# Meta tokens loaded eight tiles wide, x in eight pieces, and residual rows stored block by block from GpSimd's queue

## The chip, the cores and the metric

The kernel runs on one core of one Trainium2 chip. A core has five engines that run their own instruction streams: TensorE (PE; its weight loads are listed as PEld), VectorE (DVE), ScalarE (ACT), GpSimd (POOL) and SyncE (SP). SP issues nearly all loads; POOL and ACT can issue transfers too. They are carried by the core's 16 DMA engines. The metric is device time of one launch, in microseconds (us), lower is better. A profiled execution also gives a span, from its first to its last instruction.

## What is computed

One layer of a decoder trunk: 16 learned meta tokens are put ahead of 256 tokens of x (width 2048), and the layer's output for the 256 is returned. All data are float32.

```python
h = jnp.concatenate([meta_b, x], axis=1)            # 16 + 256 tokens, 2048 wide
u = rms_norm(h, g_pre_mix[l])
proj = u @ w_in[l]                                  # 2048 x 7168
z_pool, v_conv, g_conv, gate_a, gate_b = jnp.split(proj, splits, axis=-1)
y_a = causal_multiscale_pool(z_pool, w_pool_grp[l], pool_scale[l]) @ w_pool_out[l]
y_b = conformer_conv(v_conv, g_conv, w_dw[l], b_dw[l], conv_ln_g[l], conv_ln_b[l]) @ w_conv_out[l]
m = jax.nn.sigmoid(gate_a) * y_a + jax.nn.sigmoid(gate_b) * y_b
h = h + rms_norm(m @ w_o[l], g_post_mix[l])
u = rms_norm(h, g_pre_mlp[l])
f = jnp.square(jax.nn.relu(u @ w_up[l])) @ w_down[l]
h = h + rms_norm(f, g_post_mlp[l])
return h[:, N_META:]
```

## The kernel before

**Numbers in two parts.** TensorE multiplies float32 in a faster form with fewer bits, so every operand is kept as a high and a low part: ScalarE casts the number into `hi`, VectorE subtracts that from the number and leaves `lo`. A product of two operands then takes three matmuls (high by high, high by low, low by high). Weights arrive in rooms of 1 MB called `raw...`, are split into `hi` and `lo`, and are then multiplied; when the split is done, the room is free for the next load.

**The start (L427 to L596).** The token matrix is transposed on TensorE, because a product needs the width on the partitions. `x_in` holds x as two groups of 128 tokens; `x_tile(k)` (L484) transposes 128 columns of both groups and ScalarE and VectorE turn them into the two parts of `u`, scaled by `g_pre_mix`. `meta_tiles` (L495) does the same for the meta tokens, whose rows are in `m_in`, 16 partitions of 2048 numbers: one thin transpose for each of the 16 column tiles. The result `mt` is multiplied on VectorE, and the first part of it is cast on ScalarE before x's first tile.

The first product takes the weights of 256 columns over all 2048 rows, 16 steps `k`, and runs while x and the weights still arrive. `turn_and_split(k)` (L575) issues one tile of x and one piece of weights; three tiles (`LEAD`) are turned before the first step, and each step turns the one that comes three later. Between them stand dummy transposes (`keep_warm`, L449) that write a bank nobody reads; `DUMMIES` gives their numbers, 11 ahead of everything, 2 behind the meta tokens and 1 behind the three tiles.

SP's queue is first in, first out. `X_BEHIND` (L427) says behind which rows of which weight chunk a block of x is loaded: x's first 512 columns come at once, in two pieces on two queues (L436), and three blocks of 512 follow.

On GpSimd's queue a copy (L442) waits for the last block of x; behind it stand the conv taps and the rows of small vectors, which TensorE transposes at L904.

**The middle.** Two planned stretches follow. `Plan` (L47) collects work items with an engine, a cost and the names they read and write, simulates them, and issues them in that order. The first planned stretch ends with the product by `w_o`.

**From h to the up product (L1566 to L1681).** This part is written out by hand. `norm1.finish` gives the factor of the first norm, `residual(t, n)` (L1500) writes block `n` (512 columns) of token group `t` of the new residual `h1`, in place over the copy of x loaded there. `u2_tiles` (L1571) transposes tiles of `h1` and ScalarE and VectorE split them; `up_high` and `up_low` multiply them by the first weights of `w_up`. The scale of the second norm is not yet known then; it is applied later, by `rb`.

**The second planned stretch (from L1722).** It needs the sum of squares of `h1` (`square_h1`, eight activations on ScalarE) and gives the room of `h1` to weights, so `h1` is first stored to memory, to be read back for the last residual:

```python
    def keep_h1():
        nc.sync.dma_start(kept, h1)
        room = big.tile([P, len(H_ROOMS), CK * CW], F32, tag="k8", bufs=2, name="raw_h1")
        for n, r in enumerate(H_ROOMS):
            room_of[r] = room[:, n, :]
```

The loads into rooms 5 and 6 (`raw_h1`) stand behind this store.

## Time and profile before

| what | us |
|---|---|
| median of 3 runs | 1182.91 |
| lowest and highest of them | 1181.70, 1183.52 |
| profiled execution, its own time | 1181.75 |
| its span | 1179.6 |
| mean granted TensorE clock in it | 0.997 |

In the views, a line names the source line, the engine, the operation, the tile written and the tiles read (buffer numbers left out), the shape and the count; then busy time and mean length of one. In a timeline the first two numbers are start and length in us, and the bracket is how long the engine had stood idle before and what released it. In a table of stretches the first number after the limits is the length, then come the busy time and number of instructions of PE, PEld, DVE, ACT and POOL, the granted clock, the share of the DMA engines that was busy, and GB/s. In a list of transfers the last number is the median time in us from issue to landing.

### The profile page before, as it was taken

The page shows a single profiled execution, that of the slowest core. Times are in us where ns is not written, and L with a number is a line of the kernel's source. Part 1 is how long each engine was busy: PE and PEld are TensorE (multiplying, and loading weights), DVE is VectorE, ACT ScalarE, POOL GpSimd, SP SyncE. Part 2 cuts the span into 40 slices and gives each one's busy share as a digit, 9 for nine tenths or more (in the row PEclk, how much of TensorE's full clock was granted, in tenths as well). Part 3 has the DMA queues.
Part 4 walks back from the last instruction along what each step waited for, and adds up shares of the span by engine and source line. Part 5 has one row for each costly group of instructions (what it writes and reads, how often), then busy time and mean ns, then how long its engine had stood idle before and what let it go on. Part 6 is the DMA issues. An engine that isn't in the chain of part 4 may idle for free.

```text
span 1179.6 us, 15795 instructions
## 1 busy us (share of the span) xinstructions
PE 1167.2 (99%) x6314; PEld 1013.1 (86%) x6314; DVE 1064.4 (90%) x1155; ACT 706.8 (60%) x718; POOL 62.3 (5%) x62
## 2 busy tenths in 40 slices
PE   9999999999999999999999999999999999999996
PEld 9999998788888888898888888888888888888885
DVE  6799999999998998688998998998989989989857
ACT  7634454556478666566776666666656756656542
POOL 1000000000000000000101001000000010010000
PEclk9999999999999999999999999999999999999998
DMA  9855356789767799449999999999999999999941
GB/s 316 265 179 179 108 179 173 233 278 297 220 194 247 208 353 293 151 149 347 253 320 234 249 316 256 250 290 244 301 262 229 339 240 248 318 241 242 337 143 71
DMA packets 185177, 287.57 MB, mean 244 GB/s; under 512 B 4769, under 2 KB 92257, under 8 KB 184192
## 3 DMA queue, kind: packets, MB, share of 16 engines
q1 hardware_dynamic: 160784, 236.40, 58.7%
q0 software_dynamic: 23856, 49.44, 23.3%
q8 instruction: 49, 0.80, 0.3%
q10 hardware_dynamic: 464, 0.73, 0.2%
q14 instruction: 24, 0.20, 0.0%
HBM read 282.36 MB, written 4.19 MB: 243 GB/s over the span
## 4 chain that ended last, share of the span: by engine, by line
PE 95%; DVE 3%; DMA 1%; issue 1%; ACT 0%; DVEq 0%; ACTq 0%
PE bank_u L539 18%; PE bank_k L1252 16%; PE acc_up L1979 13%; PE bank_u L545 9%; PE acc_v L1252 9%; PE bank_k L534 8%; PE bank_a L1979 7%; PE bank_b L1979 5%; PE acc_v L534 4%; PE acc_up L539 1%; DVE lo L822 1%; PE bank_u L1979 1%; PE acc_up L545 1%; DMA raw_k<-in_w_in_dram 1%; PE acc_v L1512 0%
## 5 line engine op out<-in xcount | busy, mean ns | idle before, releaser
L539 PE MATMUL bank_u<-m,hi 128*128 128x512 f32 x960 | 329.6, 390 | 0.0
L545 PE MATMUL bank_u<-m,lo 128*128 128x256 f32 x960 | 265.3, 276 | 0.0
L539 PEld LDWEIGHTS bank_u<-m,hi 128*128 128x128 f32 x960 | 180.2, 188 | 38.0
L817 ACT CAST hi<-raw_p 128x2048 fp32r<-128x2048 f32 x70 | 133.8, 1912 | 111.1 <-PE bank_k L1252 28.2
L1805 DVE TENSOR_TENSOR lo<-raw_m,hi 128x2048 fp32r<-128x2048 f32 x75 | 171.6, 2288 | 18.5 <-ACT hi L1800 17.3
L545 PEld LDWEIGHTS bank_u<-m,lo 128*128 128x128 f32 x960 | 180.2, 188 | 1.6
L1800 ACT CAST hi<-raw_m 128x2048 fp32r<-128x2048 f32 x75 | 143.5, 1913 | 60.8 <-PE bank_u L539 39.3
L822 DVE TENSOR_TENSOR lo<-raw_p,hi 128x2048 fp32r<-128x2048 f32 x70 | 159.7, 2286 | 12.9 <-ACT hi L817 12.6
L1979 PE MATMUL acc_up<-hi,forms 128*128 128x512 f32 x440 | 143.9, 390 | 0.0
L1805 DVE TENSOR_TENSOR lo<-raw_h,hi 128x2048 fp32r<-128x2048 f32 x43 | 98.4, 2288 | 12.7 <-ACT hi L1800 12.3
L1800 ACT CAST hi<-raw_h 128x2048 fp32r<-128x2048 f32 x43 | 82.2, 1911 | 39.9 <-PE bank_u L539 17.7
L952 DVE SCALAR_TENSOR_TENSOR c<-a,taps,c 128x256 f32<-128x256 f32 x240 | 100.2, 478 | 0.0
L1979 PEld LDWEIGHTS acc_up<-hi,forms 128*128 128x128 f32 x440 | 82.6, 188 | 18.1 <-ACT G L2004 0.4
L534 PE MATMUL bank_k<-u_um,hi 128*128 128x272 f32 x512 | 95.2, 287 | 0.0
L1252 PE MATMUL bank_k<-hi,u_um 128*128 128x512 f32 x280 | 88.8, 389 | 0.7 <-ACT sg L1301 0.7
L1979 PE MATMUL acc_up<-lo,forms 128*128 128x512 f32 x220 | 86.0, 391 | 0.0
L1979 PE MATMUL bank_a<-hi,forms 128*128 128x512 f32 (+1 forms) x256 | 81.9, 383 | 0.0
L534 PEld LDWEIGHTS bank_k<-u_um,hi 128*128 128x128 f32 x512 | 79.7, 188 | 0.0
L534 PE MATMUL bank_k<-u_um,lo 128*128 128x272 f32 x256 | 73.3, 287 | 0.0
L1800 ACT CAST hi<-raw_c 128x2048 fp32r<-128x2048 f32 x23 | 43.9, 1908 | 41.7 <-PE bank_u L539 36.8
L1805 DVE TENSOR_TENSOR lo<-raw_c,hi 128x2048 fp32r<-128x2048 f32 x23 | 52.6, 2287 | 13.2 <-ACT hi L1800 13.2
L1979 PE MATMUL bank_b<-hi,forms 128*128 128x512 f32 (+1 forms) x200 | 63.5, 381 | 0.0
(398 smaller groups left out, 2230.6 us busy)
## 6 DMA issues: line engine op xcount, KB each, us to landing
raw_p<-in_w_in_dram SPq DMA_DIRECT2D x30, 1024.0 KB, 5.6
raw_m<-in_w_down_dram SPq DMA_DIRECT2D x25, 1024.0 KB, 8.8
raw_m<-in_w_down_dram POOLq DMA_DIRECT2D x23, 1024.0 KB, 10.2
raw_h<-in_w_up_dram SPq DMA_DIRECT2D x20, 1024.0 KB, 8.3
raw_m<-in_w_up_dram SPq DMA_DIRECT2D x17, 1024.0 KB, 8.2
raw_h<-in_w_down_dram SPq DMA_DIRECT2D x17, 1024.0 KB, 9.0
raw_c<-in_w_down_dram SPq DMA_DIRECT2D x15, 1024.0 KB, 5.2
raw_k<-in_w_in_dram SPq DMA_DIRECT2D x14, 1024.0 KB, 8.2
```

Of the source, the lines that this page charges most:

```text
L534: nc.tensor.matmul(acc, w[:, k[0], cs], act[:, k[1], a, off:], start=first and n == 0, stop=last and n == 2)
L539: nc.tensor.matmul(acc.rearrange("p (a t) -> p a t", a=2)[:, :, ts], hi[:, k[0], cs], act[:, k[1], :, off + ts.start:off + ts.stop], start ...
L545: nc.tensor.matmul(acc[:, :T], lo[:, k[0], cs], act[:, k[1], 0, off:], start=False, stop=stop, skip_group_check=True)
L817: nc.scalar.copy(box["flat"], rooms[q]())
L822: nc.vector.tensor_sub(lo, rooms[q](), f32(box["flat"]))
L952: nc.vector.scalar_tensor_tensor(C_c()[:, q, :], A_a()[:, q, i:i + T], taps[:, q, i:i + 1], C_c()[:, q, :], op0=ALU.mult, op1=ALU.add)
L1252: nc.tensor.matmul(banks[bank], a_(k, part), box[w_][:, k, :], start=opens and k == 0 and i == 0, stop=ends_ and k == CK - 1 and i == 2, s ...
L1800: nc.scalar.copy(box["flat"], raw_in(room))
L1805: nc.vector.tensor_sub(lo, raw_in(room), f32(box["flat"]))
L1979: nc.tensor.matmul(acc, forms[h][:, f, k, a_, :], box[w_][:, k, cs], start=start and k == 0 and n == 0, stop=stop and k == KH - 1 and n == ...
```

## The change

Four things change.

1. The meta tokens are loaded a second way, `m_wide`: 128 partitions that hold 8 column tiles of 16 tokens each, twice. Two full transposes replace sixteen thin ones. `m_in` is still needed for the squares; it is now loaded on GpSimd's queue, ahead of the taps, and its squares come behind all those of x.
2. x is loaded in blocks of 256 columns: the first in two pieces, seven more behind two rows of weights each.
3. Two tiles of x are turned before the first step of the first product, and two more (the third and fourth) behind it. The dummies become 12 at the start and 3 ahead of the first step.
4. `h1` is stored in five pieces from GpSimd's queue, each as soon as its blocks are written, and six of its eight squares are issued by hand between the transposes. The planned stretch has no store, and the loads into its two rooms wait for the last two squares in the plan alone.

```diff
-DUMMIES = (11, 2, 1)
+DUMMIES = (12, 3)
...
-    X_BEHIND = {(0, 4): 1, (0, 8): 2, (1, 4): 3}
+    X_COLS = CW // 2
+    X_BEHIND = {(0, 2): 1, (0, 4): 2, (0, 6): 3, (0, 8): 4, (1, 2): 5, (1, 4): 6, (1, 6): 7}
...
-    nc.sync.dma_start(m_in, meta)
+    KM = P // M
+    m_wide = tmp.tile([P, KD // KM, P], F32, tag="v", bufs=5, name="m_wide")
+    nc.sync.dma_start(m_wide, meta.rearrange("m (c k p) -> k m c p", k=KM, p=P))
     pre_rows = load_rows(nc.scalar, "g_pre_mix")
     for t, queue in enumerate((nc.scalar, nc.sync)):
-        queue.dma_start(x_in[:, t, :CW], xv[:, t, :CW])
+        queue.dma_start(x_in[:, t, :X_COLS], xv[:, t, :X_COLS])
...
+    nc.gpsimd.dma_start(m_in, meta)
     nc.gpsimd.dma_start(taps_in, w_dw)
...
-        pt = acc_tile("mt_in")[:, :KD * M].rearrange("p (k m) -> p k m", k=KD)
-        for k in range(KD):
-            nc.tensor.transpose(pt[:, k, :], m_in[:, k * P:(k + 1) * P], ident[:M, :M])
+        pt = acc_tile("mt_in")[:, :KD * M]
+        for c in range(KD // KM):
+            nc.tensor.transpose(pt[:, c * P:(c + 1) * P], m_wide[:, c, :], ident)
+        pt = pt.rearrange("p (k m) -> p k m", k=KD)
...
-    squares = [(b, t) for b in range(XB) for t in range(NT + 1)]
+    squares = [(b, t) for b in range(XB) for t in range(NT)] + [(b, NT) for b in range(XB)]
...
     meta_parts.pop(0)()
+    for k in range(2):
+        turn_and_split(k)
     keep_warm(DUMMIES[1])
-    for k in range(LEAD):
-        turn_and_split(k)
-    keep_warm(DUMMIES[2])
...
-        turn_and_split(k + LEAD)
+        for n in range(2 if k == 0 else k + LEAD, k + LEAD + 1):
+            turn_and_split(n)
...
+    def square_h1(t, n):
+        square_of(h1[:, t, block(n)], ssq2, t, n)
+
+    def keep(t, n0, n1):
+        cs = slice(n0 * CW, n1 * CW)
+        nc.gpsimd.dma_start(kept[:, t, cs], h1[:, t, cs])
...
     for n in range(2):
         residual(0, n)
+    square_h1(0, 0)
+    keep(0, 0, 2)
     last_block(0)
...
     residual(0, 2)
+    keep(0, 2, 3)
...
     both(u2_tiles(0, 1, 2 * CK, CK))
+    square_h1(0, 1)
     up_high(1, 0)
     parts_ = u2_tiles(1, 1, 0, CK)
     residual(1, 1)
+    keep(1, 0, 2)
     both(parts_)
+    square_h1(0, 2)
     up_high(2, 0)
     both(u2_tiles(1, 1, CK, CK))
+    for n in range(2):
+        square_h1(1, n)
     residual(1, 2)
+    square_h1(1, 2)
     last_block(1)
     residual(1, 3)
     residual(0, 3)
+    keep(1, 2, 4)
+    keep(0, 3, 4)
...
-    def keep_h1():
-        nc.sync.dma_start(kept, h1)
+    def rooms_of_h1():
         room = big.tile([P, len(H_ROOMS), CK * CW], F32, tag="k8", bufs=2, name="raw_h1")
...
     for t in range(NT):
-        for n in range(NB):
-            plan.add("ACT", 0.92, square_h1(t, n), writes=("junk", "ssq2"))
-    plan.add("SP", 6.0, keep_h1, reads=("ssq2",), writes=[f"raw{r}" for r in H_ROOMS])
+        plan.add("ACT", 0.92, lambda t=t: square_h1(t, NB - 1),
+                 reads=[f"raw{r}" for r in H_ROOMS], writes=("junk", "ssq2"))
```

The order of instructions at three places. First TensorE's start, before the change (`idle` are dummies, `xt` tiles of x, `acc_v` the first product):

```order
L451 MATMUL idle<-ident 128x128 x11
L421 MATMUL pv_g_pre_mix<-ident,rows_g_pre_mix 128x16
L498 MATMUL mt_in<-ident,m_in 128x16 x16
L451 MATMUL idle<-ident 128x128 x2
L488 MATMUL xt_175<-ident,x_in 128x128 x2
L488 MATMUL xt_182<-ident,x_in 128x128 x2
L488 MATMUL xt_189<-ident,x_in 128x128 x2
L451 MATMUL idle<-ident 128x128
L534 MATMUL acc_v_0_169<-u_um,hi_83 128x272 x2
```

And TensorE's start with the change:

```order
L455 MATMUL idle<-ident 128x128 x12
L421 MATMUL pv_g_pre_mix<-ident,rows_g_pre_mix 128x16
L502 MATMUL mt_in<-ident,m_wide 128x128 x2
L492 MATMUL xt_166<-ident,x_in 128x128 x2
L492 MATMUL xt_173<-ident,x_in 128x128 x2
L455 MATMUL idle<-ident 128x128 x3
L539 MATMUL acc_v_0_162<-u_um,hi_83 128x272 x2
L539 MATMUL acc_v_0_162<-u_um,lo_80 128x272
L539 MATMUL acc_v_1_163<-u_um,hi_83 128x272 x2
L539 MATMUL acc_v_1_163<-u_um,lo_80 128x272
L492 MATMUL xt_189<-ident,x_in 128x128 x2
L492 MATMUL xt_196<-ident,x_in 128x128 x2
```

Sixteen transposes of the meta tokens became two, two dummies went from before x's tiles to behind them, and the third tile stands behind the first product's six matmuls, beside the fourth.

Second, ScalarE between the transposes of h1, with the change (the rows that write `ssq_421` are the squares of h1, those that read `ht` make the high parts of the transposed tiles; before, the former stood in the plan, behind the latter):

```order
L1503 ACTIVATE acking_offset=None)_0_0_4165,ssq_421<-h_3575 128x512
L1598 ACTIVATE m<-ht_0_4187,vecs 128x128 x4
L1503 ACTIVATE acking_offset=None)_3_1_4206,ssq_mix<-acc_v_0_162 128x512
L1480 ACTIVATE q_mix<-v_mix 128x1
L1598 ACTIVATE m<-ht_4_4208,vecs 128x128 x4
L1598 ACTIVATE m<-ht_8_4250,vecs 128x128 x4
L1503 ACTIVATE acking_offset=None)_1_0_4263,ssq_421<-h_3575 128x512
L1598 ACTIVATE m<-ht_0_4281,vecs 128x128 x4
L1503 ACTIVATE acking_offset=None)_2_0_4296,ssq_421<-h_3575 128x512
L1598 ACTIVATE m<-ht_4_4314,vecs 128x128 x4
```

One square stands ahead of the first high parts, one ahead of the fourth set and one ahead of the fifth; three more follow behind it.

Third, SP's queue at the start of the second planned stretch, before the change:

```order
L351 DMA raw_4467<-in_w_up_dram 128x8x256
L1773 DMA raw_a<-in_w_up_dram 128x8x256
L1773 DMA raw_c<-in_w_up_dram 128x8x256
L1773 DMA raw_m_4479<-in_w_down_dram 128x4x512
L1773 DMA raw_m_4480<-in_w_up_dram 128x8x256
L1773 DMA raw_m_4481<-in_w_down_dram 128x4x512
L1773 DMA raw_a<-in_w_up_dram 128x8x256
L1778 DMA kept<-h_3580 128x4096
L1773 DMA raw_c<-in_w_down_dram 128x4x512
L1773 DMA raw_h_4593<-in_w_up_dram 128x8x256
L1773 DMA raw_h_4593<-in_w_down_dram 128x4x512
```

And with the change:

```order
L351 DMA raw_4479<-in_w_up_dram 128x8x256
L1800 DMA raw_a<-in_w_up_dram 128x8x256
L1800 DMA raw_c<-in_w_up_dram 128x8x256
L1800 DMA raw_m_4491<-in_w_down_dram 128x4x512
L1800 DMA raw_m_4492<-in_w_up_dram 128x8x256
L1800 DMA raw_m_4493<-in_w_down_dram 128x4x512
L1800 DMA raw_h_4530<-in_w_up_dram 128x8x256
L1800 DMA raw_h_4530<-in_w_down_dram 128x4x512
L1800 DMA raw_a<-in_w_up_dram 128x8x256
L1800 DMA raw_c<-in_w_down_dram 128x4x512
```

The store is gone from SP's queue, and the two loads into the rooms of h1 stand two loads earlier. On GpSimd's queue the five stores stand between the load of `g_mix` and the first adding load of the second stretch.

More of the change, by code (lines that the diff above doesn't have):

```diff
@@ L1491, in hybrid_block @@
     norm3 = Norm("mlp")
+    ssq2 = const.tile([P, NT, NB], F32, name="ssq2")
+    kept = dram.tile([P, NT, D], F32, name="kept")
+    H_ROOMS = (5, 6)
     def square_of(src, norm, t, n, scale=1.0):
@@ L1710, in hybrid_block @@
         room_of[2 + b] = raws.tile([P, CK * CW], F32, tag="raw", name=f"raw_m{b}")
-    kept = dram.tile([P, NT, D], F32, name="kept")
-    H_ROOMS = (5, 6)
     banks = {"u0": acc_tile("bank_u0"), "u1": acc_tile("bank_u1")}
@@ L1772, in load, with f @@
         room = room_at[r] = free_rooms.pop(0)
-        plan.add("SP", 3.15 if r[0][0] == "U" else 2.95, lambda: nc.sync.dma_start(
-            room_of[room].rearrange("p (k c) -> p k c", k=rows), src),
-            writes=(f"raw{room}",))
-    def keep_h1():
-        nc.sync.dma_start(kept, h1)
+        def f():
+            if room not in room_of:
+                rooms_of_h1()
+            nc.sync.dma_start(room_of[room].rearrange("p (k c) -> p k c", k=rows), src)
+        plan.add("SP", 3.15 if r[0][0] == "U" else 2.95, f, writes=(f"raw{room}",))
+    def rooms_of_h1():
         room = big.tile([P, len(H_ROOMS), CK * CW], F32, tag="k8", bufs=2, name="raw_h1")
@@ L1837, in hybrid_block @@
     last_use_order = list(uses)
-    ssq2 = const.tile([P, NT, NB], F32, name="ssq2")
     r2 = const.tile([P, NT], F32, name="r2")
     box2 = {}
-    def square_h1(t, n):
-        return lambda: square_of(h1[:, t, block(n)], ssq2, t, n)
     def mean2():
```

2 lines of the change are left out of this document (1 added, 1 removed).

## The prediction

> **What bounds the kernel now.** I read the busy times first, then the stretches, then the start of TensorE in order of time.
>
> ```profile
> PE 1167.2 (99%) x6314; PEld 1013.1 (86%) x6314; DVE 1064.4 (90%) x1155; ACT 706.8 (60%) x718; POOL 62.3 (5%) x62
> ...
> 0.00:9.65 9.65, 8.12 (x46) 7.45 (x46) 2.89 (x9) 3.94 (x9) 0.88 (x8) 1.00 0.80 248
> 9.65:485.00 475.35, 474.20 (x2667) 417.03 (x2666) 449.24 (x565) 277.41 (x289) 17.80 (x20) 1.00 0.73 228
> 485.00:540.00 55.00, 55.00 (x349) 49.52 (x349) 41.14 (x76) 33.53 (x67) 0.00 (x0) 1.00 0.62 201
> 540.00:1170.00 630.00, 629.89 (x3260) 539.05 (x3258) 565.87 (x496) 391.24 (x352) 43.63 (x34) 1.00 0.92 260
> 1170.00:1179.60 9.60, 0.00 (x0) 0.00 (x0) 5.24 (x14) 0.71 (x3) 0.00 (x0) 0.67 0.45 165
> ```
>
> The second column of a stretch is TensorE's busy time. From 9.65 to 1170 us it stands still for 1.15 + 0.00 + 0.11 = 1.26 us in all. So no transfer, cast or square that ends earlier between these two moments can gain more than that, and the stretch in which the residual rows are handled (485 to 540) has nothing to give at all. After 1170 TensorE has no work; the change touches nothing there. What can be gained lies in the first 9.65 us, where most of TensorE's "work" is filling. What can be lost lies anywhere that work with little slack is pushed.
>
> The start, TensorE:
>
> ```profile
> 1.35 2.61 PE L451 MATMUL idle<-ident 128*128 128x128 f32 x11 [1.35 <-POOL ident masks.py:199]
> 4.27 1.86 PE L498 MATMUL mt_in<-ident,m_in 16*128 16x16 f32 x16
> 6.54 1.49 PE L488 MATMUL xt<-ident,x_in 128*128 128x128 f32 x6
> 7.82 0.42 PE L451 MATMUL idle<-ident 128*128 128x128 f32 x1
> 8.03 0.82 PE L534 MATMUL acc_v<-u_um,hi 128*128 128x272 f32 x2
> 8.65 0.53 PE L534 MATMUL acc_v<-u_um,lo 128*128 128x272 f32 x1
> 9.51 0.39 PE L488 MATMUL xt<-ident,x_in 128*128 128x128 f32 x2
> 9.65 0.50 PE L534 MATMUL acc_v<-u_um,hi 128*128 128x272 f32 x2
> 10.48 0.39 PE L488 MATMUL xt<-ident,x_in 128*128 128x128 f32 x2
> ```
>
> The first product (k = 0, six matmuls) starts at 8.03, the second at 9.65, and from then on a step takes 10.48 - 9.51 = 0.97 us. The early matmuls run at half pace: the six transposes at 6.54 are (7.82 - 6.54) / 6 = 0.21 us apart; two transposes and 0.75 us of product fill a later step of 0.97, so there one is about 0.11. The page's clock column does not show this (it reads 1.00 from the start); the pace does. Matmuls reach full pace just before 9.5.
>
> **The change, part by part.**
>
> *Meta tokens.* Sixteen thin transposes (16 of 128 rows of the array, 1.86 us) become two full ones, 2 x 0.21 + 0.2 for the last to finish = 0.6. They begin when the transfer lands:
>
> ```profile
> DMA packets 8494, 9.48 MB, mean 316 GB/s; under 512 B 449, under 2 KB 7422, under 8 KB 8477
> ...
> x_in<-in_x_dram SPq DMA_DIRECT2D x1, 256.0 KB, 4.4
> x_in<-in_x_dram ACTq DMA_DIRECT2D x1, 256.0 KB, 4.6
> raw<-in_w_in_dram SPq DMA_DIRECT2D x2, 128.0 KB, 4.3
> m_in<-in_meta_dram SPq DMA_DIRECT2D x1, 128.0 KB, 3.2
> ```
> ```profile
> 0.74 0.39 SPq L433 DMA_DIRECT2D m_in<-in_meta_dram  x1
> 1.20 0.40 SPq L436 DMA_DIRECT2D x_in<-in_x_dram  x1
> ...
> 6.17 0.42 DVE L502 TENSOR_TENSOR mt<-mt_in,vecs 128x256 f32<-128x256 f32 x1 [1.53 <-PE mt_in L498]
> ...
> 6.63 0.35 ACT L507 CAST u_um<-mt 128x192 fp32r<-128x192 f32 x1 [3.46 <-DVE mt L502]
> 7.21 0.47 ACT L490 ACTIVATE u_um<-xt,vecs 128x256 fp32r<-128x256 f32 x1 [0.23 <-PE xt L488]
> ```
>
> Today's transfer (16 long rows) lands at 0.74 + 3.2 = 3.94. The wide one, 256 rows of 512 B, is not in the trace. Lower bound 3.94, upper bound the 128 KB weight piece in short rows, 0.74 + 4.3 = 5.04. I take 4.4, nearer the low end: it is first in the queue, and the weight pieces stand behind others. TensorE is through at 5.0 (4.5 to 5.65). VectorE's multiply and ScalarE's cast end 0.9 us later (6.98 against 6.13 today): 5.9 (5.4 to 6.5).
>
> *x.* Its first two pieces are halves of today's, so 256 KB less lie ahead of everything behind them: at 316 GB/s 0.8 us. Today they land at 5.6 and 5.8; I take 5.2 (5.0 if all of the 0.8 arrives, 5.8 if none). Transposes start there instead of at 6.54. ScalarE's first activation follows their start by 7.21 - 6.54 = 0.67: 5.9, the same moment as the cast above. The product follows that by 8.03 - 7.21 = 0.82: **6.7** (bounds 6.2 and, with the late meta, 7.3). TensorE's own queue agrees: four transposes and three dummies from 5.2 take 7 x 0.21, so 6.7. The weight piece, today at 1.65 + 4.3 = 5.95, comes some 0.8 earlier too and does not decide. First product: 1.3 us earlier.
>
> *x's third tile behind the first product.* This gives part of it back. Four transposes now stand between the products, where two do. At half pace product and transposes take (9.51 - 8.03) + 4 x 0.21 = 2.3, so the second product starts at 9.0: **0.6 us gained**. At full pace the product is held by VectorE's low part of the weights, third matmul 0.62 behind the first (8.65 - 8.03), then four at 0.125: 1.1; four transposes 0.44; second product at 8.25: **1.4 us gained**.
>
> Which pace? Early on TensorE now has full-width work except for two short holes (about 4.1 to 4.4 and 5.0 to 5.2), where it has 1.86 us of thin transposes today. That the clock follows the work is seen in the last stretch above: granted 0.67 where TensorE does nothing. I expect full pace before the product and take 1.4.
>
> The Trainium skill ("TensorE: Matmul & The Clock Gate", Part 1) says that the clock doubles after one busy window of about 3.4 us, and that the windows run freely; with full-width dummies from 1.35 on that would be early enough. The same page (Part 4) says that transposes do not count as busy: then only the products count, the pace comes as late behind the first of them as today, and the sum would be 1.0 instead of 1.4. The trace leans to neither: here transposes alone, 1.35 to 8.03, did not bring full pace, and 1.5 us of product were in when it came; but thin ones lay between.
>
> *Eight pieces.* Each step needs 128 KB of x and 128 KB of weights in 0.97 us, 270 GB/s, under the 316 above; rows of x get shorter, and the queue's order still puts each piece ahead of its step. Cost 0; it ends if x's pieces run slower than 270.
>
> *m_in again, on POOL.* Its issue precedes taps and rows; nearest price 0.5 us each.
>
> ```profile
> 17.84 0.52 POOL L414 DMA_DIRECT2D rows_pool_scale<-in_g_pre_mlp_dram  x1
> ...
> rows_pool_scale<-in_g_pre_mlp_dram POOLq DMA_DIRECT2D x1, 8.0 KB, 5.9
> ...
> 29.89 0.26 PE L904 MATMUL bank_y<-ident,rows_pool_scale 48*128 48x48 f32 x1
> ```
>
> The rows land at 17.84 + 5.9 = 23.7, some 0.7 later then, and are needed at 29.89: cost 0. The squares of m_in move behind those of x, long before they are summed.
>
> *Squares of h1 on ScalarE, earlier.* Each is 0.82 us (0.63 and 0.19):
>
> ```profile
> 528.04 0.63 ACT L1495 ACTIVATE ng_offset=None)_1_0_4503<-h 128x512 f32<-128x512 f32 x1
> 528.58 0.19 ACT L1495 ACTIVATION_READ_ACCUMULATOR ng_offset=None)_1_0_4503<-h 128x1 f32 x1
> ...
> 502.69 1.14 ACT L1583 ACTIVATE m<-ht,vecs 128x128 fp32r<-128x128 f32 x4 [2.68 <-PE ht L1577]
> 509.51 1.14 ACT L1583 ACTIVATE m<-ht,vecs 128x128 fp32r<-128x128 f32 x4 [1.48 <-PE ht L1577]
> ...
> 516.05 1.14 ACT L1583 ACTIVATE m<-ht,vecs 128x128 fp32r<-128x128 f32 x4 [3.04 <-PE ht L1577]
> ```
>
> They go into the idle times in brackets: one into 2.68, one into 1.48, one into a hole between, three (2.46) into 3.04. All fit; if one starts late by its residual, TensorE waits 0.4 at most, so the bound is 0 to 0.4. I take 0.
>
> *The rows of h1.* Five stores by POOL, 2 MB, replace one by SP. The last two (768 KB) meet the loads of w_up that SP issues from 519 on; the first of these has the least slack:
>
> ```profile
> 519.15 0.37 SPq L351 DMA_DIRECT2D raw<-in_w_up_dram  x1
> ...
> raw<-in_w_up_dram SPq DMA_DIRECT2D x1, 1024.0 KB, 6.3
> 525.48 1.91 ACT L356 CAST hi<-raw 128x2048 fp32r<-128x2048 f32 x1 [1.79 <-DMA raw<-in_w_up_dram]
> 527.42 2.29 DVE L359 TENSOR_TENSOR lo<-raw,hi 128x2048 fp32r<-128x2048 f32 x1 [1.33 <-ACT hi L356]
> ...
> 535.54 0.39 PE L539 MATMUL bank_u<-m,hi 128*128 128x512 f32 x1
> ...
> raw_m<-in_w_down_dram SPq DMA_DIRECT2D x25, 1024.0 KB, 8.8
> ...
> raw_m<-in_w_down_dram SPq DMA_DIRECT2D x1, 1024.0 KB, 17.8
> ```
>
> It lands at 525.45, its low part is ready at 529.7, and TensorE comes to it at 535.5: 5.8 us of cover. The 768 KB at 316 GB/s are 2.4 us, so the cover holds: 0. SP, rid of its store, loads the two new rooms earlier; TensorE has only 0.11 us of standstill behind 540, so that gains 0.1 at most.
>
> **Sum.** 1.4 from the start, 0 elsewhere: 1181.75 - 1.4 = 1180.35 for an execution like the profiled one (span 1179.6, 2.15 around it). That one is near the fastest of the three runs (1181.70, median 1182.91, slowest 1183.52); the median lies 1.16 above it. I carry 0.85 of this over, not all, since part of the spread should be the moment of full pace, which the change steadies: **1181.2**.
>
> **Rivals.**
>
> *A, the pace waits for products.* For: transposes alone have not brought it. Against: the thin ones are gone. If it comes at the moment it does now, 0.6 is gained; if it comes 1.4 behind the first product as now (9.4 - 8.03), at 8.1, the four transposes run at full pace and the second product starts at 8.2 + 0.44 = 8.65: 1.0. With all of the 1.16 the median is 1181.9 to 1182.3.
>
> *B, the wide load is late, and the change does not do what it says.* For: it has 256 short rows where 16 long ones were. Against: it is first in the queue. At the upper bound (product at 7.3, half pace, second product 9.6) nothing is left: 1181.75 to 1182.9. The Trainium skill ("DMA: Bandwidth & Descriptors", Rules for kernel authors) speaks for B: a transfer runs on no more engines than its slowest dimension allows, and the source here has eight outermost, so eight of sixteen would carry it. No run here shows it.
>
> *C, the stores hold up the loads.* Place: the w_up load of 519.15. In the last two rows above a load of SP that ran beside one of POOL (between 546 and 570 us) took 17.8 us, where the median for that tile is 8.8: 9.0 more. It decides from 5.8 on; at 9.0 TensorE waits 3.2, and 1181.2 becomes 1184.4, slower than before. Against: 768 KB, not a queue full of loads, and the kernel ran such pairs elsewhere with TensorE at 629.89 of 630.
>
> **Chances.** Full pace early 0.48 (1181.2, own range 1179.7 to 1182), A 0.28, B 0.12, C 0.12. 0.2% is 2.4 us, about what a measurement of this kernel can tell from no change. Below 1180.5: two thirds of the first case, since the carried-over part is soft, and a little of A: 0.36. Above 1185.3: two thirds of C, where the delay has no upper end: 0.08. Between: 0.56. The range leaves out C and the edges: 1179.7 to 1182.8.
>
> **What would show it.** Right: the first product near 6.7, the second near 8.25, then steps of 0.97; two transposes of mt_in before 5.0; TensorE at 55.0 of 55 from 485 to 540, shifted. A is seen by transposes 0.21 apart behind the first product; B by ScalarE's first cast waiting beyond 6.2 for VectorE's mt; C by idle of TensorE near 534 with a DMA as releaser. The prediction is wrong if the second product starts after 9.65, or if TensorE idles by more than 0.5 us anywhere behind 10 us where it does not now.

## The result, and the profile after

| kernel | median us | lowest to highest | runs |
|---|---|---|---|
| before | 1182.48 | 1181.59 to 1184.15 | 22 |
| after the change | 1180.49 | 1179.84 to 1182.66 | 22 |

The ratio is 0.9985, 95% interval 0.9979 to 0.9990. That is about 2 us: clear of the noise, but less than the 0.2% that the prediction counts as no change, and inside the predicted range (1181.2; 1179.7 to 1182.8). The profiled execution took 1180.17 us (span 1178.2) where 1180.35 was forecast for it. That the sum fits so closely is partly luck: two of its zeros did not hold, and a gain that it did not contain made up for them.

The table of stretches after the change:

```profile
0.00:9.65 9.65, 7.43 (x42) 6.11 (x43) 3.68 (x11) 4.71 (x12) 0.88 (x8) 1.00 0.69 206
9.65:485.00 475.35, 473.88 (x2662) 416.96 (x2662) 449.65 (x564) 277.38 (x286) 18.37 (x21) 1.00 0.74 229
485.00:540.00 55.00, 55.00 (x351) 49.44 (x350) 40.63 (x76) 33.67 (x65) 2.72 (x5) 1.00 0.75 249
```

In the first stretch the transfers run at 206 GB/s, before at 248. In the third, where POOL now issues the stores, TensorE is busy 55.00 of 55 as before. The start, TensorE in order of time (start, length, engine, line, operation, tiles, shape, count, idle time before and its releaser):

```profile
1.36 2.82 PE L455 MATMUL idle<-ident 128*128 128x128 f32 x12 [1.36 <-POOL ident masks.py:199]
...
4.37 0.44 PE L502 MATMUL mt_in<-ident,m_wide 128*128 128x128 f32 x2
4.66 0.92 PE L492 MATMUL xt<-ident,x_in 128*128 128x128 f32 x4
5.42 0.49 PE L455 MATMUL idle<-ident 128*128 128x128 f32 x3
6.38 0.62 PE L539 MATMUL acc_v<-u_um,hi 128*128 128x272 f32 x2 [0.46 <-ACT hi L356]
...
7.54 0.60 PE L492 MATMUL xt<-ident,x_in 128*128 128x128 f32 x4
7.90 0.49 PE L539 MATMUL acc_v<-u_um,hi 128*128 128x272 f32 x2
...
9.21 0.41 PE L492 MATMUL xt<-ident,x_in 128*128 128x128 f32 x2 [0.33 <-DMA x_in<-in_x_dram]
```

First product at 6.38 (6.7 forecast), second at 7.90 (8.25), and x's transposes at full pace. In the last row TensorE waits for a transfer, x's third block, which landed at 9.08. The next wait stands behind the matmul that starts at 29.71; it is called the wait at 29.7 from here on. One row each of ScalarE, VectorE and TensorE from the timeline of all engines after the change:

```profile
26.50 1.91 ACT L822 CAST hi<-raw_s0a 128x2048 fp32r<-128x2048 f32 x1 [2.98 <-DMA raw_s0a<-in_w_in_dram]
...
28.45 2.29 DVE L827 TENSOR_TENSOR lo<-raw_s0a,hi 128x2048 fp32r<-128x2048 f32 x1 [3.95 <-ACT hi L822]
...
30.79 0.39 PE L539 MATMUL bank_k<-u_um,lo 128*128 128x272 f32 x1 [0.80 <-DVE lo L827]
```

Read from the bottom up: TensorE waits for the low part, that for the high part, and that for a weight room that landed at 26.42. Before, the room landed at 23.90, and the same cast found it there:

```profile
24.66 1.91 ACT L817 CAST hi<-raw_s0a 128x2048 fp32r<-128x2048 f32 x1
```

How much earlier TensorE starts the same instruction than in the profile of before (us, the difference of the start times; the columns are moments of before):

| profile of | 9.65 | 12 | 29.5 | 35 | 230 | 246 | 600 | 1169 |
|---|---|---|---|---|---|---|---|---|
| after | 1.76 | 1.26 | 1.21 | 0.14 | 0.19 | 1.18 | 1.75 | 1.36 |

The start wins 1.76. 0.5 go at x's third block, and almost all the rest at 29.7. Then 1.0 comes back between 230 and 246, where two short waits of before are missing; the steps behind that are smaller. The experiments were made on these four places.

### The profile page after: what moved, and what is told of

The parts are those of the page before. It is cut to its first block, busy times and chain, and to the rows that moved or that the text cites. A ratio compares the mean times of both kernels' runs of the same rounds, so it can differ in the third digit from the quotient of the medians.

```text
span 1178.2 us, 15806 instructions
## 1 busy us (share of the span) xinstructions
PE 1164.8 (99%) x6301; PEld 1010.6 (86%) x6301; DVE 1064.7 (90%) x1155; ACT 707.5 (60%) x718; POOL 65.6 (6%) x68
## 4 chain that ended last, share of the span: by engine, by line
PE 96%; DMA 2%; DVE 1%; SPq 0%; ACT 0%; issue 0%; DVEq 0%; ACTq 0%
PE bank_u L544 18%; PE bank_k L1257 18%; PE acc_up L2000 13%; PE acc_v L1257 10%; PE bank_u L550 9%; PE bank_k L539 8%; PE bank_a L2000 7%; PE bank_b L2000 5%; PE acc_v L539 3%; PE acc_up L544 1%; DMA raw_s0a<-in_w_in_dram 1%; PE bank_u L2000 1%; PE acc_up L550 1%; DMA raw<-in_w_in_dram 1%; PE acc_v L1527 0%; PE bank_k L1527 0%
```

## The experiments

They ran in three groups, each beside runs of the kernel before on the same chip. Their medians of before differ (1182.74, 1182.84, 1183.61), so a kernel is compared by its difference to its own group's.

| kernel | median us | minus before | ratio, 95% interval |
|---|---|---|---|
| head_only | 1180.87 | -1.87 | 0.9984, 0.9975 to 0.9993 |
| store_only | 1182.62 | -0.12 | 0.9998, 0.9990 to 1.0007 |
| before_13 | 1183.06 | +0.32 | 0.9998, 0.9989 to 1.0007 |
| m_in_sp | 1180.24 | -2.50 | 0.9980, 0.9971 to 0.9989 |
| fetch_shift | 1181.43 | -1.41 | 0.9988, 0.9979 to 0.9997 |
| no_m_in | 1180.05 | -2.79 | 0.9978, 0.9969 to 0.9987 |
| wide16 | 1181.07 | -1.77 | 0.9987, 0.9978 to 0.9996 |
| x_on_act | 1180.07 | -2.77 | 0.9975, 0.9966 to 0.9984 |
| both | 1180.80 | -2.81 | 0.9979, 0.9970 to 0.9987 |
| both_x1 | 1180.01 | -3.60 | 0.9970, 0.9959 to 0.9981 |
| x_wide | 1181.40 | -2.21 | 0.9983, 0.9974 to 0.9992 |
| thin_dummies | 1180.41 | -3.20 | 0.9975, 0.9966 to 0.9985 |

The ratio is not the quotient of the two medians, so the two columns can differ a little (before_13). The intervals are about 1 us to either side, so the verdicts below rest on places in the profiles; the medians only support them. Each kernel has one profile.

### Start alone, stores alone

head_only is before with the diff's parts on the start; store_only is before with the rest.

> The changed start (wide meta load, x in eight pieces, third tile behind the first product) with the residual rows stored and squared as before. Theory: the whole gain comes from the start, 1.75 us at the second product, less 0.5 given back at x's third block and 0.8 at about 29.7 us; so about 1.2 to 2.0 below the kernel before (1180.5 to 1181.3), second product near 7.9, and TensorE's short waits for VectorE between 230 and 245 us come or stay away by themselves. Rival: those waits (0.4 and 0.3 us in the profile of before, none after) go away because of the block by block stores; then this kernel keeps them and ends 1.0 us later than the changed one, 1181.5.

> The start of before with the five stores by GpSimd and the six squares by hand. Theory: TensorE is never idle where the rows are handled, so 0 (within 0.4 of the kernel before, 1182.5), TensorE busy 55.0 of 55 between 485 and 540 us, second product at 9.65 as before. Rival: the stores are what took the waits near 233 and 242 us away: about 1.0 faster (1181.5). Other rival: they hold up a load of w_up: slower by 1 us or more.

The start carries the gain (-1.87 of -1.99); the stores are worth nothing either way (0.9998). In head_only's profile the waits near 234 and 243 are absent, in store_only's they are there, so they go with the start and not with the stores. store_only, the same stretch:

```profile
485.00:540.00 55.00, 55.00 (x347) 49.44 (x346) 41.67 (x76) 34.98 (x69) 2.72 (x5) 1.00 0.70 235
```

And TensorE's start in it:

```profile
10.01 0.80 PE L534 MATMUL acc_v<-u_um,hi 128*128 128x272 f32 x2
...
11.77 0.50 PE L534 MATMUL acc_v<-u_um,hi 128*128 128x272 f32 x2
```

Its second product starts at 10.01 and its third at 11.77, with the same start as before (9.65 and 10.62): full pace came later, and that cost 1.1 us. So the start of before is not the same in each execution, and the expectation's 9.65 was one case of it.

### The pace: two more dummies, and thin ones

```diff
-DUMMIES = (11, 2, 1)
+DUMMIES = (13, 2, 1)
```

> The kernel before with 13 dummy transposes at the start in place of 11, nothing else. Theory: about 2.8 us of unbroken full-width transposes bring TensorE to full pace, products or not, and 11 of them (2.6 us) were just too few before the thin ones broke the row: full pace near 4.2 instead of 9.3, first product near 7.4, second near 8.6, about 1.0 faster (1181.5). Rival 1 (only products count, or only the wide meta load allows it): pace comes near 9.3 again, 0 to 0.2 slower (1182.6). Rival 2: it comes early and the thin transposes lose it again: 0 to 0.5 faster.

```profile
1.36 3.04 PE L451 MATMUL idle<-ident 128*128 128x128 f32 x13 [1.36 <-POOL ident masks.py:199]
...
4.45 1.41 PE L498 MATMUL mt_in<-ident,m_in 16*128 16x16 f32 x16
...
7.42 0.62 PE L534 MATMUL acc_v<-u_um,hi 128*128 128x272 f32 x2 [0.44 <-ACT hi L356]
...
8.72 0.49 PE L534 MATMUL acc_v<-u_um,hi 128*128 128x272 f32 x2
```

In this execution the products came close to where the theory had them (7.42 and 8.72; 1180.95 us, the fastest run of this kernel), though full pace came at 5.12 and not near 4.2. The median did not move, so most runs probably do not get it; only one was profiled. The trace's record of the granted clock gives a reason. Full pace lasts 1163.945 or 1167.358 us in every profile, 341 or 342 times 3.413: it switches at the ends of windows of 3.413 us, and these lie at another phase in each execution. With TensorE's starts in the 14 profiles one can work out how much of each window was filled with full-width work (128 rows; a matmul counts until the next one, and no longer than its pitch):

| profile | windows that did not count | window behind which full pace came |
|---|---|---|
| before | 2.47 to 5.88: 38% | 5.88 to 9.29: 86% |
| store_only | 1.51 to 4.92: 65%; 4.92 to 8.34: 63% | 8.34 to 11.75: 88% |
| before_13 | | 1.70 to 5.12: 73% |
| after | | 0.75 to 4.16: 75% |
| head_only | to 3.13: 51% | 3.13 to 6.54: 81% |
| m_in_sp | | 1.81 to 5.23: 88% |
| fetch_shift | to 3.18: 52% | 3.18 to 6.60: 80% |
| no_m_in | 0.56 to 3.97: 75%; 3.97 to 7.38: 75% | 7.38 to 10.80: 93% |
| wide16 | to 2.83: 42% | 2.83 to 6.25: 87% |
| x_on_act | | 1.95 to 5.37: 78% |
| both | 0.60 to 4.01: 75%; 4.01 to 7.42: 64% | 7.42 to 10.84: 93% |
| both_x1 | | 2.40 to 5.82: 88% |
| x_wide | 0.43 to 3.84: 71% | 3.84 to 7.26: 75% |
| thin_dummies | 1.76 to 5.17: 28% | 5.17 to 8.58: 84% |

Windows filled to 78% and more always counted, to 71% and less never, and between these both happened. store_only's windows, with 0.23 us of idle at most but thin transposes in a fifth and in over a third of them, did not count: thin work fills little. In after the window that counted holds no full-width work but dummy transposes. And after's early pace is no certainty: no_m_in starts TensorE nearly as after does, and its windows of 75% did not count.

Then the dummies were made thin (four matmuls that use 16 rows; they last 2.07 us, where the twelve transposes last 2.82 and the expectation had 2.9):

```diff
-    keep_warm(DUMMIES[0])
+    for _ in range(4):
+        nc.tensor.matmul(idle[:, :P], ident[:M, :], ident[:M, :], start=True, stop=True)
```

> The changed kernel with its 12 dummy transposes at the start (128 rows of the array, 2.8 us) replaced by four matmuls that use 16 of the 128 rows and fill about the same 2.9 us. Theory: TensorE's pace doubles at the end of a 3.41 us window of which some 80% is filled with full-width work, transposes included; thin work does not fill it. Then no window counts that starts before about 3.6, full pace comes between 7.0 and 10.8 instead of 4.2 to 7.4, the second product starts at 8.1 to 9.0, and the median is 0.4 to 0.9 slower than the changed kernel (1181.2). Rival: any work on TensorE fills a window; pace before 7.4, the time of the changed kernel (1180.5).

The pace came at 8.58, as the theory had it, but the time is no worse than that of the changed kernel: a miss. The profile shows where the loss went. The second product starts 0.76 us later than in after:

```profile
8.66 0.50 PE L540 MATMUL acc_v<-u_um,hi 128*128 128x272 f32 x2
```

By 12 us TensorE is only 0.50 behind after, since it has no wait for x's third block. The wait at 29.7 is shorter too (0.57 where after has 0.96, from one matmul's start to the next less its pitch), and by 35 us it is 0.09 behind. What is lost or won ahead of 29.7 meets the landing of raw_s0a there.

### The second load of the meta tokens

m_in_sp issues it on SP's queue behind the third weight chunk. no_m_in drops it and takes the sum of squares from m_wide, where each token's numbers lie in eight partitions; the matrix `fold`, made of sums of the identity's columns, adds the eight.

```diff
     for _ in range(FIRST + 1):
         open_chunk()
+    nc.sync.dma_start(m_in, meta)
...
-    nc.gpsimd.dma_start(m_in, meta)
```

> The changed kernel with m_in loaded on SP's queue behind the third weight chunk, not on GpSimd's ahead of the taps. Theory: m_in's 16 packets of 8 KB on GpSimd's queue slow the load stream between 21 and 24 us; without them raw_s0a lands near 25.3 instead of 26.4 and TensorE's wait for lo at 29.7 (0.8 to 0.96 us) shrinks to 0.3 or less: 0.6 to 0.9 faster than the changed kernel (1179.7). Rival: the 128 KB themselves or the taps behind them cost the time; then raw_s0a lands at 26 or later and the time is that of the changed kernel, 1180.5.

```diff
+    nc.gpsimd.memset(ssq[:M, NT, 1:], 0.0)
+    fold = big.tile([P, M + 1], F32, tag="a", name="fold")
+    fold, ssq_wide = fold[:, :M], fold[:, M:]
+    nc.vector.reduce_sum(fold, ident.rearrange("p (k m) -> p m k", m=M), axis=mybir.AxisListType.X)
...
-    nc.gpsimd.dma_start(m_in, meta)
...
-    squares = [(b, t) for b in range(XB) for t in range(NT)] + [(b, NT) for b in range(XB)]
+    squares = [(0, NT)] + [(b, t) for b in range(XB) for t in range(NT)]
...
+        nc.scalar.activation(junk[:, :KD // KM * P], m_wide.rearrange("p c q -> p (c q)"), AF.Square,
+                             accum_out=ssq_wide)
...
+            nc.tensor.matmul(idle[:M, P:P + 1], fold, ssq_wide, start=True, stop=True)
+            nc.vector.tensor_copy(ssq[:M, NT, :1], idle[:M, P:P + 1])
```

> The changed kernel without the second load of the meta tokens: the sum of their squares is taken from m_wide (one square of 256 columns on ScalarE, one small matmul that adds the eight partial sums of each token). Theory: the 128 KB in 16 packets of 8 KB hold the load stream at half its rate for 2 us wherever they stand (129 and 184 GB/s from 21.5 on in the changed kernel, 185 and 191 from 19.5 on with m_in on SP's queue); without them raw_s0a lands near 25.2 instead of 26.4, TensorE's wait at 29.7 is 0.2 or less, 0.8 faster than the changed kernel (1179.7). Rival: the taps and rows on GpSimd's queue do it, or the start's slow transfers alone; then raw_s0a lands later than 25.8 and at least 0.4 of the wait stays (1180.2 or more).

The stretch from 21.2 to 24 us in after, then in no_m_in, then 19.5 to 21.5 in m_in_sp (last number: GB/s):

```profile
21.20:24.00 2.80, 2.80 (x22) 2.62 (x21) 2.80 (x6) 2.32 (x5) 0.00 (x0) 1.00 1.06 201
```
```profile
21.20:24.00 2.80, 2.80 (x23) 2.66 (x22) 2.18 (x6) 2.80 (x8) 0.00 (x0) 1.00 1.11 314
```
```profile
19.50:21.50 2.00, 2.00 (x19) 2.00 (x18) 1.59 (x5) 1.92 (x6) 1.01 (x2) 1.00 1.07 188
```

The DMA engines are busy all the time (1.06 and 1.07), but move 201 and 188 GB/s instead of 314. In after 15 of the load's 16 packets of 8 KB start between 21.19 and 21.38 and one at 23.10, and they last only 0.37 to 0.67 us each; yet the load slows what moves beside it, on GpSimd's queue as on SP's. On SP's queue the loss only came earlier, behind the third chunk's last rows:

```profile
22.57 1.66 ACT L356 CAST hi<-raw 128x512 fp32r<-128x512 f32 x3 [1.15 <-DMA raw<-in_w_in_dram]
```
```profile
23.24 0.51 PE L539 MATMUL bank_k<-u_um,hi 128*128 128x272 f32 x2 [0.45 <-ACT hi L356]
```

So the queue, the theory of m_in_sp, was wrong, and the load itself, its rival, right (the median is not worse: by 35 us this profile stands only 0.3 behind after's). Without the load raw_s0a landed at 25.13 (25.2 expected). So 1.3 of the 2.5 us by which the room is later than before are this load's. Of the other 1.2, 0.9 belong to the slower transfers at the start (next section): with the load dropped and x's first pieces on ScalarE's queue (the kernel both, below) the room landed at 24.22. In no_m_in TensorE comes to the room's low part without a wait:

```profile
27.15 2.29 DVE L835 TENSOR_TENSOR lo<-raw_s0a,hi 128x2048 fp32r<-128x2048 f32 x1 [1.01 <-ACT hi L830]
```
```profile
31.11 0.52 PE L544 MATMUL bank_k<-u_um,hi 128*128 128x272 f32 x2
31.47 0.28 PE L544 MATMUL bank_k<-u_um,lo 128*128 128x272 f32 x1
```

This profile had its full pace only at 10.80, so it is 1.6 behind after's at 29.5 and cannot show what the missing wait is worth; the median is 0.8 better against its own before than after's (-2.79 against -1.99), within the noise of both.

### The first transfers

x_on_act issues x's first block in two pieces and the second block on ScalarE's queue and moves the third one forward by two weight rows; wide16 loads m_wide in two halves with 16 rows outermost; x_wide has blocks of 512 columns behind the first 512.

```diff
-X_BEHIND = {(0, 2): 1, (0, 4): 2, (0, 6): 3, ...
+X_BEHIND = {(0, 2): 2, (0, 6): 3, ...
...
-    for t, queue in enumerate((nc.scalar, nc.sync)):
-        queue.dma_start(x_in[:, t, :X_COLS], xv[:, t, :X_COLS])
+    for t in range(NT):
+        nc.scalar.dma_start(x_in[:, t, :X_COLS], xv[:, t, :X_COLS])
+    load_x(1, nc.scalar)
```

> The changed kernel with x's first three pieces (all 512 first columns) issued on ScalarE's queue, which is idle then, and the third block moved up behind the second weight row. Theory: the early pieces are small (128 KB each) and SP issues one per 0.45 us, so SP's issuing holds the transfers to 223 to 246 GB/s between 4.5 and 6.5 us; with two queues x's third block lands before 8.6 instead of 9.1, TensorE does not wait at 9.2, and the load stream is 0.5 us ahead from there on: 0.5 to 0.9 faster (1179.8). Rival: short rows of x as such (1 KB instead of 2 KB) are what is slow; then the rate stays under 260 GB/s and the time is that of the changed kernel within 0.3 (1180.5).

```diff
-    nc.sync.dma_start(m_wide, meta.rearrange("m (c k p) -> k m c p", k=KM, p=P))
+    for c in range(KD // KM):
+        nc.sync.dma_start(m_wide[:, c, :], meta[:, c * KM * P:(c + 1) * KM * P].rearrange("m (k p) -> m k p", p=P))
...
-        pt = pt.rearrange("p (k m) -> p k m", k=KD)
+        pt = pt.rearrange("p (c m k) -> p c k m", c=KD // KM, m=M)
...
-        nc.vector.tensor_mul(mt, pt, vecs[:, g0:g0 + KD, None].broadcast_to([P, KD, M]))
+        nc.vector.tensor_mul(mt.rearrange("p (c k) m -> p c k m", k=KM), pt,
+                             vecs[:, g0:g0 + KD, None].broadcast_to([P, KD, M])
+                             .rearrange("p (c k) m -> p c k m", k=KM))
```

> The changed kernel with m_wide loaded in two halves whose source has 16 rows outermost, so that 16 DMA engines carry each half; the columns come out of the transposes in another order, which VectorE's multiply reads by strides. Theory: in the changed kernel eight engines carry the 256 packets and land at 4.3 us; with 16 the load lands 0.3 to 0.6 earlier, but TensorE is then busy with its dummies until 4.2 and x's second block sets the third step, so 0 to 0.3 faster (1180.3). Rival: the eight busy engines are what slows x and the weights behind (223 and 246 GB/s between 4.5 and 6.5 us); then x's third block lands near 8.5 instead of 9.1, the wait at 9.2 goes and the loads behind come 0.5 earlier: 0.8 faster (1179.7).

```diff
-    X_BEHIND = {(0, 2): 1, (0, 4): 2, (0, 6): 3, (0, 8): 4, (1, 2): 5, (1, 4): 6, (1, 6): 7}
+    X_BEHIND = {(0, 2): (1, 2), (0, 4): (2, 4), (0, 8): (4, 6), (1, 4): (6, 8)}
...
-        sl = slice(b * X_COLS, (b + 1) * X_COLS)
+        sl = slice(b[0] * X_COLS, b[1] * X_COLS)
```

> The changed kernel with x's first 512 columns as there (two pieces and a block of 256 columns) and the rest in three blocks of 512 columns, rows of 2 KB, behind the weight rows where before has them. Theory: the length of the rows does not matter, the rate of issues and the bytes do; the third block (512 KB) lands 0.5 later than the changed kernel's (9.1), TensorE waits for 1.0 instead of 0.5 us ahead of the third step, and the stream behind is ahead by at most 0.3: 0.2 to 0.5 slower than the changed kernel (1180.8). Rival: short rows are what slows the start; then the rate between 4.5 and 9.5 us is over 320 GB/s, the block lands by 9.3, raw_s0a lands 0.5 to 1.0 earlier and the time is 0.4 faster (1180.1).

The stretch from 4.5 to 6.5 us in after, x_on_act, wide16 and x_wide:

```profile
4.50:6.50 2.00, 1.49 (x10) 0.97 (x10) 1.28 (x5) 1.20 (x4) 0.00 (x0) 1.00 0.89 235
```
```profile
4.50:6.50 2.00, 1.60 (x9) 0.96 (x9) 0.97 (x4) 0.94 (x3) 0.00 (x0) 1.00 0.96 304
```
```profile
4.50:6.50 2.00, 1.97 (x9) 1.46 (x9) 1.12 (x4) 0.99 (x4) 0.00 (x0) 1.00 0.83 246
```
```profile
4.50:6.50 2.00, 2.00 (x9) 1.60 (x9) 1.12 (x4) 0.99 (x4) 0.00 (x0) 1.00 0.56 171
```

These two microseconds vary: the six profiles whose first transfers are those of after have 170 to 235 GB/s there, so 246 and 171 say little. The stretch from 4.5 to 9.5 us is steadier; the same six have 261 to 274, and wide16 has 264. After, x_on_act and x_wide:

```profile
4.50:9.50 5.00, 4.16 (x28) 3.27 (x29) 3.42 (x10) 3.23 (x10) 0.00 (x0) 1.00 0.93 274
```
```profile
4.50:9.50 5.00, 4.29 (x27) 3.24 (x28) 2.81 (x8) 2.67 (x8) 0.00 (x0) 1.00 1.00 331
```
```profile
4.50:9.50 5.00, 4.56 (x25) 3.90 (x25) 3.13 (x9) 2.81 (x8) 0.00 (x0) 1.00 0.76 256
```

With a second queue that issues, the same short rows run at 331 GB/s (349 and 332 in both and both_x1 below). x's third block landed at 8.32 instead of 9.08, in part because it stands further ahead in the queue, and TensorE does not wait for it. So the issues are what is slow. SP's queue in after:

```profile
1.58 0.42 SPq L439 DMA_DIRECT2D x_in<-in_x_dram  x1
2.06 0.90 SPq L351 DMA_DIRECT2D raw<-in_w_in_dram  x2
3.00 0.43 SPq L432 DMA_DIRECT2D x_in<-in_x_dram  x1
```

The pieces from 1.58 to 3.00 have 128 KB each, and SP issues one in 0.47 us; by an estimate from these rows that is 280 GB/s at most from SP. wide16 says the same from the other side. Its load runs on 16 engines (the first half lands with 16 events; of m_wide 8 events came between 3.53 and 4.32) and is whole at 4.42 where m_wide was at 4.32, so the engines were not the limit. But the one issue more puts all that stands behind 0.5 to 0.7 later, and x's second and third blocks are waited for (0.36 and 0.57 us): a miss. x_wide's rival, that short rows are slow, needed over 320 GB/s and got 256. The larger third block came at 10.64, a full 1.0 later than its theory had it:

```profile
10.77 0.41 PE L492 MATMUL xt<-ident,x_in 128*128 128x128 f32 x2 [1.63 <-DMA x_in<-in_x_dram]
```

Its median is not the worse for it against its own before (-2.21, after -1.99); TensorE has no wait at 29.7 in it. So the forecast loss of 0.2 to 0.5 did not show: a miss.

### 13 matmuls put back

Before, first in the timelines of ScalarE and of TensorE, then in the list of transfers between 205.5 and 212 us:

```profile
212.22 1.91 ACT L817 CAST hi<-raw_k 128x2048 fp32r<-128x2048 f32 x1 [1.51 <-DMA raw_k<-in_w_in_dram]
```
```profile
234.28 0.50 PE L1252 MATMUL acc_v<-lo,forms_u 128*128 128x512 f32 x1 [0.25 <-DVE lo L822]
...
242.95 0.50 PE L1252 MATMUL acc_v<-lo,u_um 128*128 128x512 f32 x1 [0.17 <-DVE lo L822]
```
```profile
q8 instruction: 1, 0.02, 1.0%
issues: line engine op xcount, KB each, median us to landing
raw_k<-in_w_in_dram SPq DMA_DIRECT2D x2, 1024.0 KB, 7.6
```

And after:

```profile
210.90 1.92 ACT L822 CAST hi<-raw_k 128x2048 fp32r<-128x2048 f32 x1 [0.32 <-PE acc_v L1257]
```
```profile
raw_k<-in_w_in_dram SPq DMA_DIRECT2D x2, 1024.0 KB, 6.6
```

Before, one packet of queue q8 lies in this stretch: 16 KB at 209.97, 1.05 us long. The page counts 49 such packets, and 6314 matmuls with as many weight loads: 258 instructions to a packet, so I read it as TensorE's program being fetched. After, this fetch falls at 212.6, behind the landing of the first room, and the two rooms land 1.0 sooner after their issue. The new start has 13 matmuls fewer (17 for 30, dummies counted). fetch_shift puts 13 back, thin, into the wait at 29.7:

```diff
-            for q in range(KC):
+            for q in [i % KC for i in range(13)] + list(range(KC)):
```

> The changed kernel with 13 thin transposes of the conv taps issued once more ahead of the real ones, near 28.9 us, just before TensorE stands still there for 0.8 to 0.96 us; 13 is the number of matmuls by which the change shortened TensorE's program ahead of this place, and they take about 0.83 us, so they fit into that wait. Theory: the 1.0 us that the changed start wins between 230 and 246 us comes from TensorE's own instruction fetch (one packet of 16 KB, 1.0 to 1.2 us on one DMA engine): before, it falls at 210 us into the load of raw_k and makes it land 1.2 us late; after, with 13 matmuls fewer, it falls at 212.6, behind that landing. With the 13 put back it falls near 210 again, raw_k lands late, TensorE's waits near 234 and 243 us come back, 0.8 to 1.0 slower than the changed kernel (1181.4). Rival: those waits have to do with the time at which the loads run, not with the count of instructions; then the fetch stays near 212.6 and the time is the changed kernel's, 1180.5.

```profile
212.37 1.91 ACT L822 CAST hi<-raw_k 128x2048 fp32r<-128x2048 f32 x1 [1.61 <-DMA raw_k<-in_w_in_dram]
```
```profile
243.28 0.50 PE L1257 MATMUL acc_v<-lo,u_um 128*128 128x512 f32 x1 [0.38 <-DVE lo L827]
```
```profile
q8 instruction: 1, 0.02, 0.8%
```

The fetch is back in the load (at 208.3), the room is late again, and so is TensorE. The median is 0.9 above the changed kernel's (0.6 against each one's before). All 14 profiles fall in line: where the fetch lies inside the first raw_k load (before, store_only, before_13, fetch_shift; 206.3 to 211.1), that load took 6.3 to 6.6 us from issue to landing, and TensorE waits near 243; in the other ten it came at 212.0 or later, the load took 5.1 to 5.4, and neither wait is there. That the fetch's moment decides these waits is shown; how one packet delays the load was not measured.

### Together

both joins no_m_in and x_on_act. both_x1 leaves x's first block as in after, moves only the second one to ScalarE's queue, and has one dummy more ahead of the first product.

```diff
-DUMMIES = (12, 3)
+DUMMIES = (12, 4)
...
+    load_x(1, nc.scalar)
```

> The changed kernel with no second load of the meta tokens (as in no_m_in) and x's first three pieces on ScalarE's queue (as in x_on_act). Theory: one takes 1.3 us out of the load stream at 21 us, the other 0.5 to 0.9 at the start; each alone gave 0.4 in the median, and where one removes the wait at 29.7 the other can only win ahead of 10 us (third block of x) and at later waits: 0.5 to 0.8 faster than the changed kernel, 1179.8. Rival: both paid for the same wait and nothing else; then 1180.05, that of either.

> As both, but of x only the second block goes on ScalarE's queue (the first block's second piece stays on SP's), and four dummies instead of three stand ahead of the first product. Theory: x's first block is whole at 5.0 again instead of 5.5, the first product starts at 6.4 to 6.6 instead of 6.73, and the fourth dummy fills the hole ahead of it, so that a window of 3.41 us that ends between 6.7 and 7.6 counts as busy too: 0.1 to 0.3 faster than both (1179.6). Rival: SP's issuing is then late again by one piece (0.45 us), x's third block lands after 9.0, TensorE waits there: the time of both or 0.2 more (1180.0).

both gained nothing over its parts, as its rival had it. In its profile x's second piece landed at 5.61 and TensorE stood still for 0.43 ahead of its transposes, which left the window from 4.01 to 7.42 at 64%: full pace at 10.84. In both_x1 TensorE waits for no transfer and no room ahead of 200 us but for the first product's weights (0.47); it is 2.43 ahead of before at the end, where after is 1.36 ahead, and has the lowest ratio of all, 0.9970. Its interval overlaps that of the change (0.9979 to 0.9990), so it is probably better and not proven so.

## Why the prediction was right, and where it was not

By the second of its own two signs of being wrong the prediction is wrong: TensorE stands idle for 0.80 us ahead of 30.79, where it does not before. The first sign did not come (second product at 7.90). So the start came out as reasoned, or better; what the prediction says of the path behind 10 us failed, and the time fits only because terms that it did not have cancelled there.

- **Meta tokens, x, first product.** Right: 4.32, 4.62 and 4.99 for the landings forecast at 4.4 and 5.2, and a second product 0.35 earlier than said. The first product waited for the weights' high part (0.46), not for x; the prediction had said that the weight piece does not decide.
- **Full pace early, and A.** Right, and A fell: transposes alone brought it at 4.16, 2.2 us ahead of the first product. The Trainium skill ("TensorE: Matmul & The Clock Gate", Part 4) says that transposes do not count as busy in the same way; this trace disagrees. Its Part 1 (free windows of 3.4 us) agrees with the 3.413 above. That pace came this early in the profiled execution was in part luck: in no_m_in's, after nearly the same start, it came at 10.80.
- **Eight pieces: "Cost 0; it ends if x's pieces run slower than 270."** Wrong by 0.5, and by its own condition: between 4.5 and 6.5 us the transfers ran at 235 GB/s. The step compared the need with the mean rate of all transfers, where the rate at which one queue issues small pieces was the limit.
- **m_in again, on POOL: "cost 0".** Wrong by up to 1.0, the wait at 29.7. The step followed the rows behind m_in on its queue (the last landed at 26.38, in time) and not the loads beside it. 1.3 of the 2.5 us of the room's delay come from it; most of the rest comes from the slower transfers at the start, which the sum put at 0 as well.
- **B.** Its mechanism is there: m_wide's data land with 8 events, as the Trainium skill's rule ("DMA: Bandwidth & Descriptors", Rules for kernel authors) has it; its price is not, since first in the queue it was whole at 4.32.
- **Squares, stores, C.** Right at 0.
- **What the sum lacked.** 1.0 us between 230 and 246 from the instruction fetch. The prediction put nothing of the 1.26 us of standstill behind 9.65 into its sum, and took 1.26 for the most that could be won there. Both were wrong: from 35 to 600 us TensorE wins 1.6. The rows of the two waits show 0.42 of idle, but by the starts of the matmuls behind them 1.0 was lost, so idle times in rows are too small a bound.
- **The 0.85 carried over.** Too large. The median after lies 0.32 above the profiled run; before, with 22 runs, 0.73 and not 1.16. Nor did the change steady the runs: they spread over 2.6 us before and 2.8 after.

In short: +1.76 at the start, -0.5 and -1.07 given back by 35 us, +1.0 by chance of where a fetch falls, and the rest in small steps (0.6 won up to 600, 0.4 lost behind it), one of them a wait near 625 us of 0 to 1.1 that differs from kernel to kernel and was not pursued.

## What to carry to other kernels

An earlier start is worth only what the load stream behind it can follow: look up the next room's landing before counting the gain, and price a small load by what it does to the transfers beside it, not by its own queue. At the start count issues as well as bytes; here an idle engine's queue raised the rate and wider rows did not. A change of a few TensorE instructions moves every later instruction fetch, so gains or losses of 1 us far behind an edit can come from there. And a total that fits can hide terms that cancel: compare the start times of the same instructions along the whole trace.

## What the hardware showed that was not expected

- Full pace switches at the ends of free windows of 3.413 us that were filled to about three quarters with full-width work, transposes included; 16-row work fills little. In store_only's profile this made 1.1 us of difference at the same instructions as before.
- A load of 128 KB in 16 rows of 8 KB held the transfers at 188 to 201 GB/s for 2 to 3 us, on either queue, with the DMA engines busy throughout; by an estimate from the 314 GB/s without it, its 128 KB alone would take 0.4 us. Why was not settled.
- A 16 KB packet, read as TensorE's instructions, lasted 1.05 us in before and 0.9 to 1.4 at this place in the other profiles; where it fell inside a 1 MB load, the load took 6.3 to 6.6 us instead of 5.1 to 5.4.
- One queue's issues limited the start: 261 to 274 GB/s between 4.5 and 9.5 us with SP issuing nearly all, 331 to 349 with ScalarE's queue as well.
